# A hybrid DeltaNet / gMLP block on one core: the first MLP product's operands in two fp16 parts in place of two float32r parts

## The chip, the core and the metric

The kernel runs as one launch on one core of one Trainium2 chip. The metric is the device time of that launch in microseconds (us), lower is better. TensorE (PE in the profile) multiplies; VectorE (DVE), ScalarE (ACT) and GpSimd (POOL) do the elementwise work; SyncE (SP) issues every DMA of this kernel, in one queue and in program order.

## What is computed

One block of a diffusion backbone on 128 context rows and 2048 latent rows of width 1024, that is 17 row tiles of 128. Cut to what matters here:

```python
h = rmsnorm(x, norm_mix) * (1 + sc1) + sh1
o = mixer(h, ...)                  # projections, chunked DeltaNet scans (both directions), gMLP, output projection
x = x + ga1 * o
h = rmsnorm(x, norm_ffn) * (1 + sc2) + sh2
x = x + ga2 * (square(relu(h @ w_ff1)) @ w_ff2)     # w_ff1: 1024 x 4096, w_ff2: 4096 x 1024
y = rmsnorm(x, norm_final)
```

All inputs and outputs are float32. The change is in `h @ w_ff1`, the first MLP product.

## The kernel before, in words

Single matmuls do not keep enough bits, so every large product is made of three: each operand is split into a high part and a low part (the rest), and `mm3` (L296, its three matmuls are L301, L302 and L303) adds high x high, high x low and low x high in PSUM. The input projections hold the parts as float16 (`split16`, L202; two parts in one tile), after both operands were scaled by powers of two that the chip works out from bounds of the data (`powers`, L221). The output projection and both MLP products hold them as float32r, unscaled, in two tiles.

The program has five stages that follow one another on TensorE:

1. The input projections with the convolution, block by block (to about 410 us), and the modulation vectors, whose weights pass through the four `raw` buffers of pool `sp` (`NS = 4`).
2. A lead-in to the scan. The last block's decay values `gcol` are transposed (L767), stored to `g_d` (L772), and loaded again as row tiles `gb` (L1082). From these ACT makes the decay matrix E (L1144), POOL and DVE the matrix that is to be inverted, DVE its first transposed factor Y (L1178), and the first product of the inversion on TensorE is L1196, `Y,AH`. Meanwhile TensorE does "fill": the projections of gate, u and v with the rows `hrow` as stationary and the fp16 weights `w` as moving operand. At most `NF = 54` steps of fill stand ahead of the scan.
3. The forward scan over 17 tiles (to about 850 us), with fill between its steps.
4. The backward scan (to about 1190 us), with the output projection as fill, and for rows 9 to 16 the second RMSNorm (`h2_steps`). That makes, for every pair of row tiles, seven combinations of the rows (Strassen's: `put`, L991), splits each in two and stores the parts to `hop_d` (L998).
5. The MLP. The first product runs as 2 x 16 units (`Unit`) of seven combinations each: a unit loads its w_ff1 block, forms the seven combinations of the weights, splits each (`split4`, L1635: ACT cast L1638, DVE subtraction L1632), and multiplies with the loaded `hop` tiles, 12 matmuls of 128x512 a combination. Weights are made `LEAD = 6` combinations ahead. Results leave PSUM by ACT copies (L1707, L1711, L1718, L1735) or DVE additions. The context tile has no pairs; its 64 steps (`context_steps`) run among the units of the second half. Then comes the second product in the same manner.

The order on each engine isn't that of the code. The code gives each step a time (`at`, `spread`, with the scan tile as unit), and the scheduler of the language orders the instructions of each engine by its own estimate. On the chip each engine runs its list in order, so that an instruction that waits holds up all behind it. On SP a load waits there for its buffer too.

Of the kernel before, what the change touches and what calls it, by code (L numbers as in the profile page):

```python
# [62 lines left out]
def hybrid_step(  # L63
# [20 lines left out]
    def f32(ap):  # L84
        return ap.bitcast(F32)
# [20 lines left out]

        return dst[tiles].rearrange("a p d -> p a d")

    hop_d = {(g, o): dp.tile([P, 4, 2, 4, P], F32, name=f"hop_{g}_{o}_d") for g in range(2) for o in range(1, 8)}
# [103 lines left out]
    done = {}  # L213
    phase = {}
    scales = cp.tile([P, 32], F32, name="scales")
    power, under, st3, uses = scales[:, 0:7], scales[:, 7:14], scales[:, 14:20], scales[:, 20:25]
    group = {1: 0, 0: 1, 2: 2, "g": 3, "v": 4, "u": 5, "ab": 6}
    def largest(out, src, axis=mybir.AxisListType.X):
# [26 lines left out]

# [118 lines left out]
    with ExitStack() as ph:  # L364
# [417 lines left out]
        def second_mods():  # L782

            load(out=wsT, in_=w_spatialT)
            V.tensor_copy(wscale[:, 0:4], vec[:, 68:69].to_broadcast([P, 4]))
            mrow = wp.tile([32, P], F32, tag="w", name="mrow4")
            load(out=mrow, in_=mod_d[:, 3 * D : 5 * D].rearrange("c (a b) -> c a b", b=P))
            pc = pt()
            T.transpose(pc[:, 0:32], mrow, ident[:32, :32])
            pc4 = pc[:, 0:32].rearrange("p (c a k) -> p c a k", c=2, a=2)  # L790
            V.tensor_copy(b2, pc4[:, :, 0, :])
            for cd in range(2):
                V.scalar_tensor_tensor(out=a2[:, cd, :], in0=pc4[:, cd, 1, :], scalar=1.0, in1=vec[:, 24:32],
                                       op0=ALU.add, op1=ALU.mult)

        mods = [st for jc in range(4, 10) for st in mod_steps(jc, p1)]
        blk, xs_, cols = prep_block(0)
# [145 lines left out]
    def h2_steps(t, psum, tmp, wide=w512, part=None, half=None, src=None):  # L943
# [1 line left out]

        u = {}
        cd = cond(t)
        wide, part, half = wide, part or wide, half or w512

        def rows():  # L950
            u["x"] = [wide("x"), wide("x")]
# [88 lines left out]
    def hop_tile(dt, n):  # L1040

        side, bufs = ("A", 2) if n else ("B", 5)
        return hops[side].tile([P, 4, 2, 4, P], dt, tag="hop", name="hop", bufs=bufs)

    def hop_next():
        g, o = hop_order.pop(0)
        hop[g, o] = t = hop_tile(F32R, o in ORDER[:2])
        for k in range(0, 4, 2):
            load(out=f32(t)[:, k : k + 2], in_=hop_d[g, o][:, k : k + 2])


    with ExitStack() as ph:
# [355 lines left out]
        def fpart(name):  # L1408
            return fp.tile([P, 512], F32, tag="part", name=name, bufs=5)

        def fhalf(name, dt):
            return sp.tile([P, 512], dt, tag="raw", name=name)


        WO = []
# [215 lines left out]
    def add(out, a, b, op=ALU.add):  # L1631
        V.tensor_tensor(out=out, in0=a, in1=b, op=op)  # L1632

    def split4(src, name="w"):

        h = wp.tile([P, 4, P], F32R, tag="w", name=name + "H")
        lo = wp.tile([P, 4, P], F32R, tag="w", name=name + "L")
        A.copy(h, src)  # L1638
# [11 lines left out]
    class Unit:  # L1650
# [14 lines left out]
        def weights(self, o):  # L1665

            a, w, t = self.raw, self.w, self.t
            if o == 1:
                w[1] = split4(a[0, 0])
            elif o == 5:  # L1670
                t["s"] = as4(w512("s"))
                add(t["s"], a[1, 0], a[1, 1])
                w[5] = split4(t["s"])
            elif o == 6:
                add(t["s"], t["s"], a[0, 0], ALU.subtract)
                w[6] = split4(t["s"])
            elif o == 7:
                d = as4(w512("d"))
                add(d, a[0, 0], a[1, 0], ALU.subtract)
                w[7] = split4(d)  # L1680
            elif o == 3:
                add(t["s"], a[0, 1], t["s"], ALU.subtract)
                w[3] = split4(t["s"])
            elif o == 2:
                w[2] = split4(a[0, 1])
            else:
                w[4] = split4(a[1, 1])

        def product(self, o, onto=None):
            if onto is None:  # L1690
# [11 lines left out]
        def step(self, o):  # L1702
            ps, t = self.ps, self.t
            if o == 1:
                self.product(1)
                t["x"] = w512("x")
                A.copy(t["x"], ps[1])  # L1707
            elif o == 5:
                self.product(5)
                t["p5"] = w512("p5")  # L1710
                A.copy(t["p5"], ps[5])  # L1711
            elif o == 6:
                self.product(6)
                add(t["x"], ps[6], t["x"])
            elif o == 7:
                self.product(7)
                t["z22"] = z = w512("p7")
                A.copy(z, ps[7])  # L1718
                add(z, z, t["x"])
                add(z, z, t["p5"])  # L1720
                rl2(z, z)
                self.out(1, 1, z)
            elif o == 3:
                self.product(3, 5)
                c = w512("c12")
                add(c, ps[5], t["x"])
                rl2(c, c)
                self.out(0, 1, c)
                t["s1"] = w512("s1")
                add(t["s1"], c, t["z22"])  # L1730
                self.keep(s1_d, t["s1"])
            elif o == 2:
                self.product(2, 1)
                c = w512("c11")
                A.activation(c, ps[1], AF.Relu)  # L1735
                A.activation(c, c, AF.Square)
                self.out(0, 0, c)
                s2 = w512("s2")
                add(s2, t["s1"], c, ALU.subtract)
                self.keep(s2_d, s2)  # L1740
            elif o == 4:
                self.product(4, 7)
                c = w512("c21")
                add(c, ps[7], t["x"])
                rl2(c, c)
                self.out(1, 0, c)

    def first_load():
        for i in range(2):
            r = as4(w512("x0"))  # L1750
            load(out=r, in_=h2_d[0][:, i * 4 : i * 4 + 4, :])
            h, lo = split4(r, "x")
            x0.extend((h[:, k, :], lo[:, k, :]) for k in range(4))

    def context_steps(m):
# [5 lines left out]
            u["raw", m] = raw_w(w_ff1[0, k * P : (k + 1) * P, fb * 512 : fb * 512 + 512])  # L1761

        def split():
            u["w", m] = split_w(u.pop(("raw", m)))

        def product():
            if k == 0:
                u["ps"] = bank()
            mm3(u["ps"], [x0[k] + u.pop(("w", m))], first=k == 0, last=k == KT - 1)
            if k == KT - 1:  # L1770
                u["r", fb] = w512("r0")
                A.activation(u["r", fb], u["ps"], AF.Relu)
# [405 lines left out]
```

## Time and profile before

| | us |
|---|---|
| median of 3 runs | 2526.11 (2523.6 to 2528.16) |
| the profiled execution | 2525.39 |
| its span, first to last instruction | 2523.7 |
| TensorE busy | 2482.3 (98%) |
| VectorE busy | 1865.2 (74%) |
| ScalarE busy | 1267.1 (50%) |

The clock granted to TensorE is 0.996 of full speed over the span. Matmuls are pipelined: the duration of one in the profile (some 380 ns for 512 columns) is longer than the distance between the starts of two that follow each other, so a stage's rate is read from the starts in the timeline, and a busy share near 100% can hide short gaps.

### The profile page before, as it was taken

The page shows a single profiled execution, that of the slowest core. Times are in us where ns is not written, and L with a number is a line of the kernel's source. Part 1 is how long each engine was busy: PE and PEld are TensorE (multiplying, and loading weights), DVE is VectorE, ACT ScalarE, POOL GpSimd, SP SyncE. Part 2 cuts the span into 40 slices and gives each one's busy share as a digit, 9 for nine tenths or more (in the row PEclk, how much of TensorE's full clock was granted, in tenths as well). Part 3 has the DMA queues.
Part 4 walks back from the last instruction along what each step waited for, and adds up shares of the span by engine and source line. Part 5 has one row for each costly group of instructions (what it writes and reads, how often), then busy time and mean ns, then how long its engine had stood idle before and what let it go on. Part 6 is the DMA issues. An engine that isn't in the chain of part 4 may idle for free.

```text
span 2523.7 us, 44015 instructions
## 1 busy us (share of the span) xinstructions
PE 2482.3 (98%) x15182; PEld 1917.2 (76%) x15182; DVE 1865.2 (74%) x3877; ACT 1267.1 (50%) x3129; POOL 231.9 (9%) x428
## 2 busy tenths in 40 slices
PE   9999999999999999999999999999999999999998
PEld 4666667666666787788888888888888888888887
DVE  4868886877778889886678878777775557685775
ACT  3756764555556667753455535444343333243442
POOL 3112212211111111110000000000000000000000
PEclk9999999999999999999999999999999999999999
DMA  8766756544444658785977899666589979786773
GB/s 293 231 182 212 226 162 192 178 150 135 129 145 156 217 172 272 260 268 174 313 225 238 249 313 297 188 192 181 145 287 374 324 262 332 243 261 203 225 265 109
DMA packets 479334, 566.61 MB, mean 225 GB/s; under 512 B 37684, under 2 KB 284764, under 8 KB 475526
## 3 DMA queue, kind: packets, MB, share of 16 engines
q1 hardware_dynamic: 479110, 563.80, 68.8%
q8 instruction: 119, 1.95, 0.3%
q14 instruction: 105, 0.86, 0.1%
HBM read 392.90 MB, written 170.76 MB: 223 GB/s over the span
## 4 chain that ended last, share of the span: by engine, by line
PE 84%; DVE 7%; DMA 4%; ACT 2%; issue 1%; SPq 1%; POOL 1%; POOLq 0%; DVEq 0%; ACTq 0%
PE f L301 16%; PE f L303 16%; PE f L302 16%; PE pj L301 6%; PE pj L302 6%; PE pj L303 6%; PE pd L1116 4%; DMA QK<-qk_d 2%; PE pm L301 1%; PE pm L303 1%; PE pm L302 1%; PE pt L671 1%; DMA raw<-in_w_ff_dram 1%; PE pt L630 1%; PE pm L425 1%
## 5 line engine op out<-in xcount | busy, mean ns | idle before, releaser
L301 PE MATMUL f<-hop,zH 128*128 128x512 f32 (+1 forms) x976 | 376.2, 386 | 1.2 <-ACT zH L1638 1.2
L302 PE MATMUL f<-hop,zH 128*128 128x512 f32 (+1 forms) x976 | 376.1, 386 | 0.0
L303 PE MATMUL f<-hop,zL 128*128 128x512 f32 (+1 forms) x976 | 376.1, 386 | 0.0
L301 PE MATMUL f<-hop,wH 128*128 128x512 f32 x896 | 349.7, 391 | 1.6 <-ACT p L1711 1.4
L302 PE MATMUL f<-hop,wH 128*128 128x512 f32 x896 | 348.7, 389 | 0.0
L303 PE MATMUL f<-hop,wL 128*128 128x512 f32 x896 | 347.3, 389 | 0.0
L1638 ACT CAST zH<-zraw 128x512 fp32r<-128x512 f32 x240 | 146.9, 621 | 294.0 <-DMA zraw<-s_d 92.4
L301 PEld LDWEIGHTS f<-hop,zH 128*128 128x128 f32 x976 | 183.3, 188 | 38.6 <-ACT zH L1638 1.6
L303 PEld LDWEIGHTS f<-hop,zL 128*128 128x128 f32 x976 | 183.3, 188 | 37.2 <-DVE zL L1632 0.4
L302 PEld LDWEIGHTS f<-hop,zH 128*128 128x128 f32 x976 | 183.3, 188 | 36.9 <-issue 0.2
L1632 DVE TENSOR_TENSOR zL<-zraw,zH 128x512 fp32r<-128x512 f32 x240 | 162.8, 687 | 65.3 <-ACT zH L1638 53.5
L301 PEld LDWEIGHTS f<-hop,wH 128*128 128x128 f32 x896 | 168.2, 188 | 37.2 <-ACT p L1711 2.3
L303 PEld LDWEIGHTS f<-hop,wL 128*128 128x128 f32 x896 | 168.2, 188 | 35.2
L302 PEld LDWEIGHTS f<-hop,wH 128*128 128x128 f32 x896 | 168.3, 188 | 34.6
L301 PE MATMUL pj<-kH,w 128*128 128x386 f16 (+2 forms) x568 | 180.3, 321 | 6.0 <-ACT w L205 3.3
L302 PE MATMUL pj<-kL,w 128*128 128x386 f16 (+2 forms) x568 | 181.2, 322 | 0.0
L303 PE MATMUL pj<-kH,w 128*128 128x386 f16 (+2 forms) x568 | 180.1, 321 | 0.0
L181 POOL TENSOR_TENSOR r<-rsq,nhalf 128x1 f32<-128x1 f32 (+1 forms) x37 | 25.2, 682 | 1386.4 <-DVE rsq L180 1386.4
L1638 ACT CAST wH<-s 128x512 fp32r<-128x512 f32 x96 | 59.4, 621 | 123.3 <-DVE s L1632 116.8
L617 DVE SCALAR_TENSOR_TENSOR cv<-pj,vec,cv 128x384 f32<-128x384 f32 (+2 forms) x142 | 82.9, 588 | 26.7 <-ACT cv L615 25.5
L301 PE MATMUL pj<-w,hrow 128*128 128x512 f16 x248 | 94.0, 379 | 0.0
L303 PE MATMUL pj<-w,hrow 128*128 128x512 f16 x248 | 94.0, 379 | 0.0
(447 smaller groups left out, 5526.0 us busy)
## 6 DMA issues: line engine op xcount, KB each, us to landing
zraw<-z_d SPq DMA_DIRECT2D x212, 256.0 KB
raw<-in_w_ff_dram SPq DMA_DIRECT2D x192, 256.0 KB
hop<-hop_d SPq DMA_DIRECT2D x28, 1024.0 KB
z_d<-c SPq DMA_DIRECT2D x96, 256.0 KB
zraw<-s_d SPq DMA_DIRECT2D x96, 256.0 KB
raw<-in_w_mod_dram SPq DMA_DIRECT2D x80, 256.0 KB
r<-in_w_ff_dram SPq DMA_DIRECT2D x80, 256.0 KB
s_d<-s SPq DMA_DIRECT2D x64, 256.0 KB
```

The costliest lines, as they stand in the source:

```text
L181: G.tensor_tensor(out=out, in0=t[:np_, :n], in1=nhalf[:np_, :n], op=ALU.pow)
L301: T.matmul(ps, lh, rh, start=first and i == 0, stop=False, skip_group_check=more)
L302: T.matmul(ps, lh, rl, start=False, stop=False, skip_group_check=more)
L303: T.matmul(ps, ll, rh, start=False, stop=last and i == n - 1, skip_group_check=more)
L425: T.matmul(pm[0:2, :], scond[:, k, :], raws[k], start=k == 0, stop=k == KT - 1)
L617: V.scalar_tensor_tensor(out=cv, in0=ps[:, w : w + ncol - 2], scalar=convw[:, w, j : j + 1], in1=cv, op0=ALU.mult, op1=ALU.add)
L630: T.transpose(pq[:, i * P : (i + 1) * P], u["x2"][i], ident)
L671: T.matmul(ps[:, i * P : (i + 1) * P], kTt[:, i * P : (i + 1) * P], rhs[i], start=True, stop=True)
L1116: T.matmul(p[:, h, :], lhs[:, h, :], rhs[:, h, :], start=True, stop=True)
L1632: V.tensor_tensor(out=out, in0=a, in1=b, op=op)
L1638: A.copy(h, src)
```

## The change

Both operands of the first MLP product are split into float16 parts instead of float32r parts, and are scaled for that:

- The rows' scale: `second_mods` takes the largest absolute values of the modulation tables `a2` and `b2`, makes a power of two of them (`four_sum_power`, `powers`: two small matmuls, some column operations on DVE) and multiplies `a2` and `b2` by it.
- The weights' scale: all of w_ff1 is read once more, in 64 loads of 256 KB through the same four `raw` buffers of pool `sp`, and ACT squares each in place with the row sums added up (`square_w1`). `w1_range` then makes the power of two.
- A weight combination is split by an ACT activation with a scale column and a DVE scalar_tensor_tensor (`split16x4`), in place of the ACT cast and the DVE subtraction. Both parts share one tile.
- PSUM is scaled back where it leaves: ACT copies get a scale column, DVE additions become scalar_tensor_tensor (`add_scaled`).
- `put` stores both parts, now 2 bytes an element, with one DMA of 256 KB in place of two of 256 KB. A `hop` tile now holds the parts for both halves of the rows, so that the second half's load no longer waits for a buffer.
- The products' number and shapes stay: 2688 matmuls of 128x512 in the units and 192 in the context steps.

The core of the diff:

```diff
-    hop_d = {(g, o): dp.tile([P, 4, 2, 4, P], F32, ...
+    hop_d = {(g, o): dp.tile([P, 4, 2, 4, P], F16, ...
+    def square_w1(n, raw):
+        A.activation(raw, raw, AF.Square, accum_out=w1_sums[:, n : n + 1])
+
+    def four_sum_power(s, r, top, psum, squared):
+        V.tensor_scalar_mul(top, top, 16.0 if squared else 4.0)
+        powers(s, r, top, 1, psum, squared)
...
+            largest(parts[:, 0:1], a2, mybir.AxisListType.XY)
+            largest(parts[:, 1:2], b2, mybir.AxisListType.XY)
+            V.scalar_tensor_tensor(out=top, in0=parts[:, 0:1], scalar=32.0, in1=parts[:, 1:2], op0=ALU.mult, op1=ALU.add)
+            four_sum_power(h2_power, h2_under, top, pt, False)
+            V.tensor_scalar_mul(a2, a2, h2_power)
+            V.tensor_scalar_mul(b2, b2, h2_power)
...
-            h, lo = half("opH", F32R), half("opL", F32R)
-            A.copy(h, src)
-            V.tensor_tensor(out=lo, in0=src, in1=f32(h), op=ALU.subtract)
-            for i, piece in enumerate((h, lo)):
-                store(out=dst[:, i], in_=f32(piece).rearrange("p (k d) -> p k d", k=4))
+            pair = half("op")
+            A.copy(pair[:, 0, :], src)
+            V.tensor_tensor(out=pair[:, 1, :], in0=src, in1=pair[:, 0, :], op=ALU.subtract)
+            store(out=dst, in_=pair.rearrange("p i (k d) -> p i k d", k=4))
...
+        def w1_load(n):
+            k, fb = divmod(n, 8)
+            w1_raws[n] = raw_w(w_ff1[0, k * P : (k + 1) * P, fb * 512 : fb * 512 + 512], sp, "raw")
...
+        for n in range(64):
+            at(0.5 + n * 0.24, lambda n=n: w1_load(n))
+            at(1.0 + n * 0.24, lambda n=n: square_w1(n, w1_raws.pop(n)))
+        at(16.5, w1_range, "fill")
...
+    def split16x4(src, scale=None):
+
+        t = wp.tile([P, 2, 4, P], F16, tag="w", name="w16")
+        h, lo = t[:, 0], t[:, 1]
+        if scale is None:
+            A.copy(h, src)
+            add(lo, src, h, ALU.subtract)
+        else:
+            A.activation(h, src, AF.Copy, scale=scale)
+            V.scalar_tensor_tensor(out=lo, in0=src, scalar=scale, in1=h, op0=ALU.mult, op1=ALU.subtract)
+        return h, lo
...
+    def add_scaled(out, ps, b):
+        V.scalar_tensor_tensor(out=out, in0=ps, scalar=mlp_under, in1=b, op0=ALU.mult, op1=ALU.add)
...
-                w[1] = split4(a[0, 0])
+                w[1] = split(a[0, 0])
...
-                A.copy(t["x"], ps[1])
+                A.activation(t["x"], ps[1], AF.Copy, scale=mlp_under)
...
-                add(t["x"], ps[6], t["x"])
+                add_scaled(t["x"], ps[6], t["x"])
```

In the code the 64 loads and squares are spread over the forward scan. The scheduler puts them earlier: all 64 stand between the last block of the projections and the first steps of the scan. Three places show it.

On TensorE, in the lead-in, at the transposes of the decay values `gcol` (`hrow` is stationary fill, `w` its moving weights). Before:

```order
L301 LDWEIGHTS hrow
L301 MATMUL pm<-w_2997,hrow 128x512
L767 MATMUL pt<-ident,gcol 128x128
L768 MATMUL pt<-ident,gcol 8x128
L302 LDWEIGHTS hrow
L302 MATMUL pm<-w_2997,hrow 128x512
```

Changed (L313 to L315 are the three matmuls of `mm3`, L779 and L780 the two transposes):

```order
L314 LDWEIGHTS hrow
L314 MATMUL pj<-w_3244,hrow 128x512
L779 MATMUL pt<-ident,gcol 128x128
L780 MATMUL pt<-ident,gcol 8x128
L315 LDWEIGHTS hrow
L315 MATMUL pj<-w_3244,hrow 128x512
```

111 fill matmuls stand before the first scan product `Y,AH` in both. Before, 25 of them stand ahead of `gcol` and 86 behind it; now 92 stand ahead and 19 behind.

On SP, from the store of the decay values to the loads of `gb`. Before:

```order
L772 DMA g_d<-scr 128x128
L773 DMA g_d<-scr 8x128
L1369 DMA gate_d<-th 128x512
L635 DMA vt_d<-tk 128x2x128 x3
L1082 DMA gb<-g_d 128x512 x2
```

Changed (L187 are the new loads of w_ff1):

```order
L187 DMA raw<-in_w_ff_dram 128x512 x3
L784 DMA g_d<-scr 128x128
L785 DMA g_d<-scr 8x128
L373 DMA hrow<-h_d 128x768 x2
L647 DMA vt_d<-tk 128x2x128
L1391 DMA gate_d<-th 128x512
L647 DMA vt_d<-tk 128x2x128
L373 DMA hrow<-h_d 128x768 x2
L647 DMA vt_d<-tk 128x2x128
L373 DMA hrow<-h_d 128x768 x5
L1104 DMA gb<-g_d 128x512 x2
```

Nine loads of `hrow` now stand between the store and the loads that read it back, and 40 of the 64 new loads stand ahead of the store.

On ACT, from the first steps of the scan's first two tiles (L1144/L1166 make E, L1170/L1192 cast AH, L1212/L1234 and L1213/L1235 take Y and X out of PSUM). Before:

```order
L1170 CAST AH<-KK 128x512
L1344 ACTIVATE gw<-pm,scales 128x512
L1347 ACTIVATE gw<-gw,scales 128x512
L1344 ACTIVATE gw<-pj,scales 128x512
L1212 CAST Y<-pd 128x16x16
L1213 CAST X<-pd 128x16x16
```

Changed (L247 are the new squares):

```order
L1192 CAST AH<-KK 128x512
L247 ACTIVATE raw,w_sums<-raw 128x512 x3
L1366 ACTIVATE gw<-pm,scales 128x512
L247 ACTIVATE raw,w_sums<-raw 128x512 x4
L1369 ACTIVATE gw<-gw,scales 128x512
L247 ACTIVATE raw,w_sums<-raw 128x512 x3
L1366 ACTIVATE gw<-pj,scales 128x512
L247 ACTIVATE raw,w_sums<-raw 128x512
L1234 CAST Y<-pd 128x16x16
L1235 CAST X<-pd 128x16x16
```

Eleven squares now stand between this cast of AH and the next Y. In all, 40 squares stand ahead of the first E of the scan and 24 behind it.

More of the change, by code (lines that the diff above doesn't have):

```diff
@@ L107, in by_tiles @@
         return dst[tiles].rearrange("a p d -> p a d")
-    hop_d = {(g, o): dp.tile([P, 4, 2, 4, P], F32, name=f"hop_{g}_{o}_d") for g in range(2) for o in range(1, 8)}
+    hop_d = {(g, o): dp.tile([P, 4, 2, 4, P], F16, name=f"hop_{g}_{o}_d") for g in range(2) for o in range(1, 8)}
     z_d = [dp.tile([4 if a else 1, P, 2, NK, P], F32, name=f"z{a}_d") for a in range(5)]
@@ L215, in hybrid_step @@
     scales = cp.tile([P, 32], F32, name="scales")
+    w1_sums = cp.tile([P, 64], F32, name="w1_sums")
+    h2_power, h2_under, w1_power, w1_under, mlp_under = (scales[:, i : i + 1] for i in range(25, 30))
     power, under, st3, uses = scales[:, 0:7], scales[:, 7:14], scales[:, 14:20], scales[:, 20:25]
@@ L289, in w512, with pair16 @@
         return wp.tile([P, 512], dt, tag="w", name=name)
+    def pair16(name):
+        return wp.tile([P, 2, 512], F16, tag="w", name=name)
     def wrow(row):
@@ L794, in second_mods @@
                                        op0=ALU.add, op1=ALU.mult)
+            top8 = smp.tile([P, 8], F32, tag="topc", name="toph", bufs=1)
+            top, parts = top8[:, 0:1], top8[:, 3:5]
+            largest(parts[:, 0:1], a2, mybir.AxisListType.XY)
[4 more added lines that the diff above has]
+            V.tensor_scalar_mul(b2, b2, h2_power)
         mods = [st for jc in range(4, 10) for st in mod_steps(jc, p1)]
@@ L947, in h2_steps @@
         cd = cond(t)
-        wide, part, half = wide, part or wide, half or w512
+        wide, part, half = wide, part or wide, half or pair16
         def rows():
@@ L1042, in hop_tile @@
         side, bufs = ("A", 2) if n else ("B", 5)
-        return hops[side].tile([P, 4, 2, 4, P], dt, tag="hop", name="hop", bufs=bufs)
+        shape = [P, 2, 4, 2, 4, P] if dt == F16 else [P, 4, 2, 4, P]
+        return hops[side].tile(shape, dt, tag="hop", name="hop", bufs=bufs)
     def hop_next():
         g, o = hop_order.pop(0)
-        hop[g, o] = t = hop_tile(F32R, o in ORDER[:2])
+        if g == 0:
+            both = hop_tile(F16, o in ORDER[:2])
+            hop[0, o], hop[1, o] = both[:, 0], both[:, 1]
         for k in range(0, 4, 2):
-            load(out=f32(t)[:, k : k + 2], in_=hop_d[g, o][:, k : k + 2])
+            load(out=hop[g, o][:, k : k + 2], in_=hop_d[g, o][:, k : k + 2])
     with ExitStack() as ph:
@@ L1409, in fpart, with fhalf, w1_range @@
             return fp.tile([P, 512], F32, tag="part", name=name, bufs=5)
-        def fhalf(name, dt):
-            return sp.tile([P, 512], dt, tag="raw", name=name)
+        def fhalf(name):
+            return sp.tile([P, 2, 512], F16, tag="raw", name=name)
+        w1_raws = {}
+        def w1_load(n):
+            k, fb = divmod(n, 8)
+            w1_raws[n] = raw_w(w_ff1[0, k * P : (k + 1) * P, fb * 512 : fb * 512 + 512], sp, "raw")
+        def w1_range():
+            top = smp.tile([P, 8], F32, tag="topc", name="topw", bufs=1)[:, 0:1]
+            row = sp.tile([P, 512], F32, tag="raw", name="row1")
+            V.memset(row[0:8, 0:P], 1.0)
+            phase["ones"] = row[:, 0:P]
+            V.tensor_reduce(out=top, in_=w1_sums, axis=mybir.AxisListType.X, op=ALU.max)
+            four_sum_power(w1_power, w1_under, top, pj, True)
+            V.tensor_tensor(out=mlp_under, in0=w1_under, in1=h2_under, op=ALU.mult)
         WO = []
@@ L1679, in weights @@
                 add(d, a[0, 0], a[1, 0], ALU.subtract)
-                w[7] = split4(d)
+                w[7] = split(d)
             elif o == 3:
                 add(t["s"], a[0, 1], t["s"], ALU.subtract)
-                w[3] = split4(t["s"])
+                w[3] = split(t["s"])
             elif o == 2:
-                w[2] = split4(a[0, 1])
+                w[2] = split(a[0, 1])
             else:
-                w[4] = split4(a[1, 1])
+                w[4] = split(a[1, 1])
         def product(self, o, onto=None):
@@ L1710, in step @@
                 t["p5"] = w512("p5")
-                A.copy(t["p5"], ps[5])
+                A.activation(t["p5"], ps[5], AF.Copy, scale=mlp_under)
             elif o == 6:
                 self.product(6)
-                add(t["x"], ps[6], t["x"])
+                add_scaled(t["x"], ps[6], t["x"])
             elif o == 7:
@@ L1717, in step @@
                 t["z22"] = z = w512("p7")
-                A.copy(z, ps[7])
+                A.activation(z, ps[7], AF.Copy, scale=mlp_under)
                 add(z, z, t["x"])
@@ L1725, in step @@
                 c = w512("c12")
-                add(c, ps[5], t["x"])
+                add_scaled(c, ps[5], t["x"])
                 rl2(c, c)
@@ L1734, in step @@
                 c = w512("c11")
-                A.activation(c, ps[1], AF.Relu)
+                A.activation(c, ps[1], AF.Relu, scale=mlp_under)
                 A.activation(c, c, AF.Square)
@@ L1763, in split @@
         def split():
-            u["w", m] = split_w(u.pop(("raw", m)))
+            u["w", m] = split16(u.pop(("raw", m)), w1_power)
         def product():
@@ L1771, in product @@
                 u["r", fb] = w512("r0")
-                A.activation(u["r", fb], u["ps"], AF.Relu)
+                A.activation(u["r", fb], u["ps"], AF.Relu, scale=mlp_under)
         def turn():
```

9 lines of the change are left out of this document (5 added, 4 removed).

## The prediction

> **What bounds the kernel now.** I read the page's busy times first, then the table of stages, the groups of matmuls in the first MLP product, and the timeline of TensorE's starts. The page:
>
> ```profile
> span 2523.7 us, 44015 instructions
> PE 2482.3 (98%) x15182; PEld 1917.2 (76%) x15182; DVE 1865.2 (74%) x3877; ACT 1267.1 (50%) x3129; POOL 231.9 (9%) x428
> ```
>
> The table by stage (lead-in, both scans, first MLP product, second; columns: length, then busy us and instructions of each engine, granted clock, DMA share, GB/s):
>
> ```profile
> 391.00:468.00 77.00, 76.72 (x581) 49.60 (x580) 52.32 (x163) 37.72 (x115) 22.45 (x16) 1.00 0.67 210
> 410.00:850.00 440.00, 429.89 (x3845) 287.47 (x3844) 336.61 (x956) 249.41 (x672) 74.45 (x84) 1.00 0.51 159
> 850.00:1180.00 330.00, 320.23 (x2749) 267.21 (x2750) 269.96 (x672) 209.73 (x664) 51.37 (x62) 1.00 0.71 235
> 1192.00:1860.00 668.00, 666.35 (x2987) 550.91 (x2986) 505.85 (x826) 316.81 (x617) 5.72 (x9) 1.00 0.74 232
> ```
>
> From 1192 to 1860 us TensorE is busy 666 of 668 us, at clock 1.00. The groups there say with what, and that almost nothing makes it wait (after the last bar: its idle time):
>
> ```profile
> L301 PE MATMUL f<-hop,wH 128*128 128x512 f32 x896 | 349.7, 391 | 1.6 <-ACT p L1711 1.4 <-DMA hop<-hop_d 0.2
> L301 PE MATMUL f<-wH,xH 128*128 128x512 f32 x64 | 25.5, 399 | 0.0
> ```
>
> With L302 and L303 that is 3 x 896 + 3 x 64 = 2880 matmuls of 128x512 in float32r. A duration of 391 ns isn't their rate; the starts are. Two rows of the timeline, 149 matmuls apart, and below them two of the fp16 fill in the lead-in, 63 apart, same shape, both at clock 1.00:
>
> ```profile
> 1466.10 0.39 PE L302 MATMUL f<-hop,wH 128*128 128x512 f32 x1
> ...
> 1499.92 0.39 PE L301 MATMUL f<-hop,wH 128*128 128x512 f32 x1
> ```
>
> ```profile
> 429.83 0.38 PE L303 MATMUL pm<-w,hrow 128*128 128x512 f16 x1
> ...
> 443.43 0.38 PE L303 MATMUL pm<-w,hrow 128*128 128x512 f16 x1
> ```
>
> 33.82 / 149 = 227.0 ns for float32r, 13.60 / 63 = 215.9 ns for float16. So this stage is paced by the matmul stream itself: 2880 x 0.227 = 654 of its 668 us.
>
> **The change, part by part.**
>
> *The products in fp16.* Their number stays, each start comes 227.0 - 215.9 = 11.1 ns sooner: 2880 x 11.1 ns = 32.0 us gained, if nothing else becomes the limit.
>
> *Splits and evictions in that stage* get a scale column. The rows to compare (cast and scaled activation; DVE subtraction and scalar_tensor_tensor; a PSUM copy and a PSUM activation with scale column):
>
> ```profile
> L1638 ACT CAST wH<-raw 128x512 fp32r<-128x512 f32 x95 | 57.7, 619 | 0.3 <-PE f L303 0.3
> L205 ACT ACTIVATE w<-raw,scales 128x512 f16<-128x512 f32 x48 | 31.8, 718 | 0.7 <-DVE w L206 0.5
> L1632 DVE TENSOR_TENSOR wL<-raw,wH 128x512 fp32r<-128x512 f32 x95 | 64.6, 684 | 11.6 <-ACT wH L1638 11.6
> L206 DVE SCALAR_TENSOR_TENSOR w<-raw,scales,w 128x512 f16<-128x512 f32 x48 | 34.0, 741 | 1.5 <-ACT w L205 1.5
> L1711 ACT COPY p<-f 128x512 f32<-128x512 f32 x32 | 18.8, 586 | 32.4 <-PE f L303 28.4 <-DVE wL L1632 4.0
> L1344 ACT ACTIVATE gw<-pm,scales 128x512 f32<-128x512 f32 x17 | 11.7, 690 | 7.7 <-PE pm L303 7.4 <-DVE bst L1375 0.2
> 1325.00:1350.00 25.00, 25.00 (x116) 20.69 (x115) 22.34 (x40) 13.35 (x30) 0.55 (x1) 1.00 0.71 226
> ```
>
> ACT: 288 splits x 99 ns = 28.5 us, 136 evictions x 104 ns = 14 us. DVE: 288 x 57 ns = 16.4 us, and 96 additions out of PSUM, for which I take the same 57 ns, 5.5 us. In a stage of 668 - 32 = 636 us ACT goes from 317 to 359 us (56%), DVE from 506 to 528 us (83%). Both stay under TensorE, and weights are made six combinations (16 us) ahead: I take 0. If that cover is gone, it is in places like the last row above, where DVE is busy 22.3 of 25 us; 22.3 x 1.04 in 25 x 0.952 us is 97%. Bound: +5.
>
> *64 loads and 64 squares in the lead-in.* Nothing like it stands there now. The prices: an accumulating square of 128x512 (two starts in a row), a 256 KB load in quiet and in dense traffic (the chain of waits, from issue to landing), and the traffic of 385 to 470 us, in 40 slices:
>
> ```profile
> 40.16 0.63 ACT L252 ACTIVATE junk<-raw 128x512 bf16<-128x512 f32 x1
> ...
> 40.91 0.63 ACT L252 ACTIVATE junk<-raw 128x512 bf16<-128x512 f32 x1
> ```
>
> ```profile
> 592.63 2.93 DMA QK<-qk_d
> ...
> 960.96 6.21 DMA QK<-qk_d
> ```
>
> ```profile
> GB/s 10 123 121 63 183 65 151 108 242 122 103 211 235 251 282 264 289 354 250 182 102 97 194 305 384 295 318 404 400 400 368 326 265 2 0 0 0 112 248 18
> ```
>
> ACT: 64 x 0.755 = 48 us on top of 37.7 in 77 us. DMA: 210 GB/s x 77 us = 16.2 MB, plus 64 x 0.262 = 16.8 MB, 33.0 MB; at the best slice, 404 GB/s, that needs 82 us. Each alone asks for 5 to 9 us more than there is. The Trainium skill's page "DMA: Bandwidth & Descriptors" (Specifications) gives about 358 GB/s as the limit of HBM for a core; by it 33.0 MB would need 92 us, 15 more than there is. The slices at 400 and 404 speak against it, and the sum goes by them.
>
> What decides is the order of the instructions. The transposes of `gcol` start a chain (store, load of `gb`, E, the matrix, Y) that the first scan product waits for:
>
> ```profile
> 424.21 0.27 PE L767 MATMUL pt<-ident,gcol 128*128 128x128 f32 x1
> ...
> 443.65 0.28 PE L1196 MATMUL pd<-Y,AH 128*128 128x64 f16 x4
> ```
>
> ```profile
> 441.35 0.70 DVE L1178 STREAM_TRANSPOSE Y<-X 128x512 f16<-128x512 f16 x1
> ```
>
> ```profile
> 425.46 0.22 PE pt L630 x2
> ```
>
> Y is there at 442.05, 17.8 us after `gcol`. Now 86 fill matmuls (18.6 us) stand between, and TensorE comes 1.6 us after Y: the chain is hidden. In the changed order only 19 stand between (4.1 us) and three pairs of transposes (0.7 us), because the other 67 went ahead of `gcol`. TensorE then stands for 17.8 - 4.8 = 13.0 us. The fill is limited and its order fixed, so nothing gives this back later.
>
> On SP, nine loads of `hrow` now stand between the store and the load of `gb`:
>
> ```profile
> 415.76 2.81 SPq L361 DMA_DIRECT2D hrow<-h_d x6
> 426.19 3.78 SPq L635 DMA_DIRECT2D vt_d<-tk x3
> ```
>
> 9 x 0.47 = 4.2 us, in part while SP would stand at the `vt_d` stores anyway (3.78 now): +2, between -3.8 (that stand is over by then) and +4.2. The 24 squares behind the first E (18 us of ACT, eleven in a row ahead of one Y) and the loads ahead of `hrow` block in order: +3, between 0 and the 12 us that ACT and DMA lack at worst. Lead-in in all: 13 + 2 + 3 = +18, between 9 and 29.
>
> *The two powers of two.* Each is two small matmuls with DVE work between them; the order puts 18 or more fill matmuls between the two: 0, at most 1 each.
>
> *Half the bytes to `hop_d`* in the backward scan, 28 stores of 256 KB in place of these 56:
>
> ```profile
> hop_d<-opH SPq DMA_DIRECT2D x28, 256.0 KB
> hop_d<-opL SPq DMA_DIRECT2D x28, 256.0 KB
> DVE QK L1216 <- DMA QK<-qk_d: 20.8, 11, 2.9
> ```
>
> That is 7.3 MB of the stage's 235 GB/s x 330 us = 77.6 MB, and DVE waits there 20.8 us for QK loads. 9.5% of that is 2 us: -2, between 0 and -8, since the QK load queues mostly behind other loads.
>
> *Sum:* -32 + 18 - 2 + 0 = -16, from the profiled execution's 2525.4 (span 2523.7 and 1.7 around it) to 2509.4. The median of the runs lies 0.7 above it: 2510. Bounds: -32 - 8 + 9 = -31, and -32 + 29 + 5 + 2 = +4: 2495 to 2530.
>
> **The rivals.**
>
> *The staging buffers pace the lead-in (slower).* A new load waits for the square four loads earlier, and SP with it. A round of four takes the landing time, an issue (0.3) and a square (0.755). At 2.93 us that is 16 x 4.0 = 64 us, which fits in 77; at 6.21 us it is 16 x 7.3 = 117 us, 40 more than there is, and all loads of the scan stand behind it: -32 - 2 + 40 = +6, 2532. It decides against the change from a round of (77 + 32) / 16 = 6.8 us on. For it: bytes in the lead-in double, and with 0.67 it is busy already. Against: TensorE's stand of 13 us is time for it. Chance 0.18.
>
> *The lead-in costs nothing:* the chain after `gcol` is short enough on the chip, or TensorE reaches `gcol` earlier than the order suggests. -34 + 1, 2492. Against it stand the 19 matmuls of cover. 0.12.
>
> *The change doesn't do what it says:* the fp16 rate of the fill doesn't hold for `hop`, whose 512 columns are four pieces, while the fill's lie in one. Then +16, 2541. Against it:
>
> ```profile
> 1182.73 0.39 PE L301 MATMUL pj<-wH,oH 128*128 128x512 f32 x1
> ...
> 1191.80 0.39 PE L302 MATMUL pj<-wL,oH 128*128 128x512 f32 x1
> ```
>
> In float32r the output projection, with columns in one piece, starts 40 matmuls in 9.07 us, 226.8 ns each, like the units. 0.04.
>
> *An fp16 stream far faster than the fill's.* It would have to be paced by something that the fill doesn't show; no row does. The Trainium skill's page "TensorE: Matmul & The Clock Gate" (Back-to-back issue gap) gives 216 ns at 512 columns for one matmul after another, which the trace agrees with (215.9), and about 131 ns for a sustained stream of weight loads and matmuls, which it does not. By the second the gain would be 2880 x 96 ns = 276 us, 2249. 0.01.
>
> **How the numbers follow.** The forecast has 0.65, the rivals the rest. 0.2% of this kernel is 5 us, about what a measurement can tell from no change. Faster by more: 0.58 of the forecast's 0.65, 0.05 of the first rival, the second and the fourth whole, 0.76. Within: 0.05 and 0.04, 0.09. Slower: 0.02, 0.09 and the third's 0.04, 0.15. The range leaves out the third and fourth rival, the upper half of the first and the forecast's and the second's edges, together under 0.2: 2493 to 2531.
>
> **What would show it right or wrong.** In the changed profile: 216 ns between starts of the units' matmuls, and a first MLP product of about 636 us; some 13 us or more in which TensorE waits ahead of the first `Y,AH`, with the later stages' lengths nearly kept; all squares done early in the scan. The sum is wrong if the lead-in's stand is under 9 or over 29 us, if the units' starts stay at 227 ns, or if DVE holds TensorE up in the units.

## The result, and the profile after

| | before | after |
|---|---|---|
| median of 4 runs, us | 2527.14 (2523.6 to 2532.5) | 2553.43 (2552.52 to 2554.16) |
| span of the profiled execution | 2523.7 | 2551.3 |
| granted TensorE clock | 0.996 | 0.988 |

The ratio is 1.0102, 95% interval 1.0083 to 1.0121: the change makes the kernel 26 us slower, where 16 us faster was forecast. One execution of those below, of e12_rows_power_fixed, ran at a granted clock of 0.849 and took 2787.75 us; it is left out of the medians. The page of after, its first two lines of busy time:

```profile
span 2551.3 us, 44102 instructions
PE 2468.6 (97%) x15188; PEld 1664.4 (65%) x15188; DVE 1888.3 (74%) x3898; ACT 1342.8 (53%) x3257; POOL 235.7 (9%) x429
```

TensorE is busy 13.7 us less than before and yet the span is 27.6 us longer. The table by stage says where (lead-in, both scans, first MLP product; columns as in the prediction's table, windows moved to where the stages now lie):

```profile
391.00:513.00 122.00, 87.51 (x593) 52.89 (x592) 54.97 (x176) 77.06 (x245) 22.46 (x15) 0.87 0.84 266
455.00:895.00 440.00, 402.05 (x3635) 269.07 (x3634) 327.09 (x932) 257.25 (x700) 63.38 (x82) 0.97 0.53 166
895.00:1225.00 330.00, 324.31 (x2778) 269.82 (x2776) 273.90 (x680) 213.42 (x670) 52.19 (x63) 1.00 0.64 207
1236.00:1884.00 648.00, 637.16 (x2985) 294.93 (x2984) 522.20 (x822) 352.38 (x616) 8.19 (x9) 0.99 0.68 207
```

What took 77 us takes 122, and TensorE is busy in 87.5 of them. The starts of the Y factor, one for each scan tile, give the same without windows: the first stands 35.1 us later than before (476.4 for 441.4), the fourth 45.2 later, and then the distance stays, 45.4 at the last tile of the forward scan. So 45 us go into the lead-in and the first three tiles, and nothing more into the forward scan. By stages, from one first instruction to the next:

| | before | after | forecast | found |
|---|---|---|---|---|
| Y of the fourth tile starts | 487.5 | 532.7 | +18 | +45.2 |
| from there to the first unit | 704.7 | 703.9 | -2 | -0.8 |
| first MLP product | 667.7 | 647.2 | -32 | -20.5 |
| second product, to the end | 663.7 | 667.5 | 0 | +3.8 |

In the lead-in, the timeline of the chain that the prediction priced at 17.8 us, across the engines:

```profile
449.75 0.33 PE L779 MATMUL pt<-ident,gcol 128*128 128x128 f32 x1 [0.54 <-ACT tk L646]
456.74 0.38 SPq L784 DMA_DIRECT2D g_d<-scr  x1
464.29 0.91 SPq L1104 DMA_DIRECT2D gb<-g_d  x2
469.38 1.28 ACT L1166 ACTIVATE E<-gb,gcol 128x128 f32<-128x128 f32 x4 [8.79 <-DMA gb<-g_d]
476.41 0.70 DVE L1200 STREAM_TRANSPOSE Y<-X 128x512 f16<-128x512 f16 x1
477.16 0.37 PE L1218 MATMUL pd<-Y,AH 128*128 128x64 f16 x4 [21.57 <-DVE Y L1200]
```

`gcol` itself comes at 449.75 in place of 424.21, 25.5 us later. From there to the start of Y it was 17.1 us and is 26.7: the store to `g_d` stands 7.0 us behind the transposes (0.7 before), since loads of w_ff1 are ahead of it on SP, and the load of `gb` another 7.5 (5.1 before). TensorE has used up its fill by then and stands 21.57 us.

In the first MLP product the waits on TensorE are these:

```profile
PE f L313 <- ACT p L1768: 7.8, 1, 7.8
PE f L1000 <- DVE x L993: 2.4, 1, 2.4
PE f L313 <- DVE tmp L1524: 0.8, 1, 0.8
```

The rate is what was forecast. Two starts of units, 95 matmuls apart:

```profile
1300.55 0.38 PE L313 MATMUL f<-hop,w 128*128 128x512 f16 x1
...
1321.05 0.38 PE L315 MATMUL f<-hop,w 128*128 128x512 f16 x1
```

20.50 / 95 = 215.8 ns (215.9 forecast). What is missing of the 32 us is one stand. The timeline around it, SP, ACT and TensorE in order of time:

```profile
1488.79 0.66 ACT L1015 CAST op<-y 128x512 f16<-128x512 f32 x1
1494.85 0.77 SPq L1006 DMA_DIRECT2D h_d<-ev  x1
1499.28 0.32 SPq L1808 DMA_DIRECT2D x<-h_d  x1
1499.69 0.38 SPq L1006 DMA_DIRECT2D h_d<-ev  x1
1502.53 0.62 ACT L1680 CAST w<-x 128x512 f16<-128x512 f32 x1 [13.08 <-DMA x<-h_d]
1503.41 0.32 SPq L1808 DMA_DIRECT2D x<-h_d  x1
1506.74 0.62 ACT L1680 CAST w<-x 128x512 f16<-128x512 f32 x1 [3.59 <-DMA x<-h_d]
1507.26 0.68 ACT L1768 ACTIVATE p<-f,scales 128x512 f32<-128x512 f32 x1
1507.99 0.59 PE L313 MATMUL f<-hop,w 128*128 128x512 f16 x1 [7.82 <-ACT p L1768]
1508.37 0.63 PE L314 MATMUL f<-hop,w 128*128 128x512 f16 x1
...
1512.21 0.46 PE L314 MATMUL f<-hop,w 128*128 128x512 f16 x1
1512.51 0.38 PE L315 MATMUL f<-hop,w 128*128 128x512 f16 x1
```

These are the context tile's rows, `x0`. They are stored to DRAM in two halves (L1006) and loaded again (L1808); each load is issued only 4.4 and 3.7 us after the store that it reads. Their splits stand on ACT's in-order list with the loads not yet there, and behind them stands the eviction `p` that TensorE needs. The same stand was there before, at 0.5 us: ACT waited 7.1 and 1.7 us for these two loads, TensorE 0.49 us for the `p` behind them. (The other 0.9 of the 1.4 us at `p` lie 70 us later.) After the stand of 7.8 us the matmuls start 9 x 0.427 us apart (1508.37 to 1512.21) and only then 0.22 apart, 2 us more. The Trainium skill's page "TensorE: Matmul & The Clock Gate" (What's actually happening; Wait — 56ns, not 53.3ns?) says that the array runs at half its clock after an idle window of some 3.4 us, with 426.7 ns between starts at 512 columns, and 215.7 when warm: the trace agrees with both figures.

### The profile page after: what moved, and what is told of

Read it like the earlier page. It is cut to its first block, busy times and chain, and to the rows that moved or that the text cites. A ratio compares the mean times of both kernels' runs of the same rounds, so it can differ in the third digit from the quotient of the medians.

```text
span 2551.3 us, 44102 instructions
## 1 busy us (share of the span) xinstructions
PE 2468.6 (97%) x15188; PEld 1664.4 (65%) x15188; DVE 1888.3 (74%) x3898; ACT 1342.8 (53%) x3257; POOL 235.7 (9%) x429
## 4 chain that ended last, share of the span: by engine, by line
PE 79%; DMA 8%; DVE 6%; ACT 4%; issue 1%; SPq 1%; POOL 1%; POOLq 0%; DVEq 0%; ACTq 0%
PE f L313 16%; PE f L314 16%; PE f L315 16%; PE pj L313 5%; PE pj L315 5%; PE pj L314 5%; PE pd L1138 5%; DMA raw<-in_w_ff_dram 2%; PE pm L313 2%; PE pm L314 2%; PE pm L315 2%; DMA QK<-qk_d 1%; PE pt L683 1%; DMA raw<-in_w_mod_dram 1%; DMA t_d<-r 1%
## 5 line engine op out<-in xcount | busy, mean ns | idle before, releaser
L313 PE MATMUL f<-hop,zH 128*128 128x512 f32 (+1 forms) x976 | 376.8, 386 | 2.1 <-ACT zH L1691 2.1
L315 PE MATMUL f<-hop,zL 128*128 128x512 f32 (+1 forms) x976 | 376.7, 386 | 0.4 <-DVE zL L1673 0.4
L313 PE MATMUL f<-hop,w 128*128 128x512 f16 x896 | 340.3, 381 | 8.6 <-ACT p L1768 7.8
L314 PE MATMUL f<-hop,w 128*128 128x512 f16 x896 | 341.2, 381 | 0.0
L315 PE MATMUL f<-hop,w 128*128 128x512 f16 x896 | 339.8, 381 | 0.0
L314 PEld LDWEIGHTS <-w 128*128 128x128 f16 x1536 | 151.3, 99 | 154.3 <-issue 16.1
L313 PEld LDWEIGHTS <-w 128*128 128x128 f16 x1536 | 151.1, 98 | 147.7 <-issue 3.8
L315 PEld LDWEIGHTS <-w 128*128 128x128 f16 x1536 | 151.2, 98 | 145.0 <-issue 3.5
L313 PEld LDWEIGHTS f<-hop,zH 128*128 128x128 f32 x976 | 183.4, 188 | 40.8 <-ACT zH L1691 3.8
L315 PEld LDWEIGHTS f<-hop,zL 128*128 128x128 f32 x976 | 183.4, 188 | 39.6 <-DVE zL L1673 2.9
L313 PE MATMUL pj<-kH,w 128*128 128x386 f16 (+2 forms) x568 | 181.1, 323 | 6.3 <-ACT w L205 3.3
L315 PE MATMUL pj<-kH,w 128*128 128x386 f16 (+2 forms) x568 | 180.1, 321 | 0.0
L181 POOL TENSOR_TENSOR r<-rsq,nhalf 128x1 f32<-128x1 f32 (+1 forms) x37 | 26.7, 720 | 1372.2 <-DVE rsq L180 1372.2
L1683 ACT ACTIVATE w<-s,scales 128x512 f16<-128x512 f32 x96 | 68.5, 717 | 94.5 <-DVE s L1673 94.2
L206 DVE SCALAR_TENSOR_TENSOR w<-raw,scales,w 128x512 f16<-128x512 f32 x112 | 81.9, 745 | 20.3 <-ACT w L205 20.3
L313 PE MATMUL pj<-w,hrow 128*128 128x512 f16 x248 | 94.5, 381 | 0.0
```

The costliest lines, as they stand in the source:

```text
L181: G.tensor_tensor(out=out, in0=t[:np_, :n], in1=nhalf[:np_, :n], op=ALU.pow)
L206: V.scalar_tensor_tensor(out=t[:, 1, :], in0=raw, scalar=scale, in1=t[:, 0, :], op0=ALU.mult, op1=ALU.subtract)
L313: T.matmul(ps, lh, rh, start=first and i == 0, stop=False, skip_group_check=more)
L314: T.matmul(ps, lh, rl, start=False, stop=False, skip_group_check=more)
L315: T.matmul(ps, ll, rh, start=False, stop=last and i == n - 1, skip_group_check=more)
L1683: A.activation(h, src, AF.Copy, scale=scale)
```

## The experiments

Theory at the start: the 64 loads and squares, in the in-order lists of SP and ACT ahead of the first scan chain, are the whole lead-in loss (A). Rivals: `gcol`'s place behind the fill costs its 13 us by itself, as the prediction had it, and the pass the rest (B); the bytes cost their time wherever they stand (C). "Pass" means the 64 loads and 64 squares. Each run's ratio is to runs of the kernel before on the same chip.

| run | median us | ratio, 95% interval |
|---|---|---|
| e1_no_pass | 2519.27 | 0.9972, 0.9961 to 0.9982 |
| e2_pass_in_before | 2556.90 | 1.0115, 1.0100 to 1.0130 |
| e3_pass_spread | 2521.49 | 0.9977, 0.9966 to 0.9988 |
| e4_gcol_early | 2538.52 | 1.0044, 1.0027 to 1.0060 |
| e5_squares_only | 2528.68 | 1.0000, 0.9990 to 1.0011 |
| e6_loads_only | 2543.86 | 1.0064, 1.0046 to 1.0083 |
| e7_spread_and_mended | 2502.39 | 0.9901, 0.9872 to 0.9931 |
| e8_other_pool | 2556.76 | 1.0117, 1.0094 to 1.0140 |
| e9_no_pass_mended | 2500.17 | 0.9889, 0.9872 to 0.9905 |
| e10_small_loads | 2528.57 | 1.0001, 0.9991 to 1.0011 |
| e11_x0_alone | 2542.33 | 1.0059, 1.0044 to 1.0074 |
| e12_rows_power_fixed | 2506.15 | 0.9919, 0.9899 to 0.9939 |

**e1_no_pass.**

```diff
-        for n in range(64):
-            at(0.5 + n * 0.24, lambda n=n: w1_load(n))
-            at(1.0 + n * 0.24, lambda n=n: square_w1(n, w1_raws.pop(n)))
+        at(0.5, lambda: V.memset(w1_sums, 0.64))
```

> The changed kernel without the 64 loads and 64 squares; the table of row sums is filled with a fixed 0.64 instead (that part of the computation is left out). The order on TensorE stays as in the changed kernel, gcol behind the fill. Theory A (the loads and squares, standing in the in-order lists of SP and ACT ahead of the first scan chain, are the whole +45 us of the lead-in): Y of the first scan tile starts at about 441 us as before the change, total 2553 - 45 = 2508. Theory B (the place of gcol behind the fill costs 13 us by itself, as the prediction had it, the pass the rest): Y at about 454, total 2521. Theory C (the traffic of the pass): as A here, 2508.

2519.27, theory B. The timeline:

```profile
433.72 0.27 PE L779 MATMUL pt<-ident,gcol 128*128 128x128 f32 x1
451.79 0.70 DVE L1200 STREAM_TRANSPOSE Y<-X 128x512 f16<-128x512 f16 x1
452.55 0.37 PE L1218 MATMUL pd<-Y,AH 128*128 128x64 f16 x4 [7.86 <-DVE Y L1200]
```

Without the pass the chain is back at 18.1 us (17.1 before), but `gcol` is still 9.5 us late and every Y of the forward scan 10.2 to 10.5. So the pass costs 2553.4 - 2519.3 = 34 us, and something else in the change 10 to 13. The expectation was wrong in one point: the order on TensorE does not stay. Of the 111 fill matmuls, 65 stand ahead of `gcol` here and 46 behind it, against 92 and 19 in the changed kernel. So the pass itself moves `gcol` too. The 40 matmuls more than before take 40 x 0.216 = 8.6 of the 9.5 us.

**e2_pass_in_before.** The kernel before with the same three lines of loads and squares added.

> The kernel before, float32r products and all, plus the 64 loads and 64 squares at the same given times (their sums are used by nothing). Theory A and theory C: the lead-in's +45 us come by themselves, 2527 + 45 = 2572. Theory B: here gcol stands between its two places (39 groups of fill ahead of it, 48 in the changed kernel, 25 before), so that a part of the 13 us is missing: about 2563. If the loss needs the fp16 part: 2527.

2556.90: +30.4 with float32r products. The pass costs its time without any fp16 in the kernel. Theory A's 45 is out; B had forecast 2563. (In the trace 39 fill matmuls stand ahead of `gcol`, as expected, but in the changed kernel it is 92, not 48.)

**e3_pass_spread.**

```diff
-            at(1.0 + n * 0.24, lambda n=n: square_w1(n, w1_raws.pop(n)))
+            at(1.0 + n * 0.24, lambda n=n: calm(lambda: square_w1(n, w1_raws.pop(n))))
```

> The changed kernel with each square ordered on ACT behind the scan step that its time stands for, so that loads and squares are spread over the forward scan, about four for each scan tile; all bytes and all squares stay. Theory A: the 45 us go and little comes back in the scan (ACT has 25 idle us in 100 there): 2508 to 2513. Theory B: 13 us stay at the first Y,AH: 2521. Theory C (16.8 MB cost their time wherever they stand): the lead-in is short but the scan grows by 30 to 45 us: 2540 to 2553.

2521.49. The same bytes and squares, at other places, cost 2 us in place of 34: theory C falls. In the traced execution Y starts with e1's at the first tile and falls 4.7 us behind over the forward scan (tile 16 at 767.4 for 762.7). SP stands long in it:

```profile
SPq L187 <- ACT raw L247: 68.9, 39, 4.0
```

That costs at most the 2 to 5 us above. That what stands behind these loads on SP is wanted later still is the likely reason; it wasn't tried.

**e4_gcol_early.** The last three of the four gate tiles of fill are ordered on TensorE behind the two transposes of `gcol`.

```diff
...
+            st = st if g == 0 else lambda st=st: after_gcol(st)
...
```

> The changed kernel with the transposes of gcol ahead of the last three of the four gate tiles of fill, about where they stand in the kernel before; the 64 loads and squares stay where they are. Theory A: SP and ACT still hold the chain up and gcol's place gives at most its few us: 2545 to 2553. Theory B: 13 us come back and the stand ahead of the first Y,AH falls from 21.6 to about 9 us: 2540. A third case: gcol's place is most of the 45 us: 2515.

2538.52, 15 us less, theory B again; 24 fill matmuls stand ahead of `gcol` here. The stand ahead of the first `Y,AH` falls to 6.4 us:

```profile
PE pd L1220 <- DVE Y L1202: 6.4, 1, 6.4
```

**e12_rows_power_fixed** asks why `gcol` is late without the pass. To e1 it adds:

```diff
-            largest(parts[:, 0:1], a2, mybir.AxisListType.XY)
-            largest(parts[:, 1:2], b2, mybir.AxisListType.XY)
...
-            four_sum_power(h2_power, h2_under, top, pt, False)
+            V.memset(h2_power, 64.0)
+            V.memset(h2_under, 1.0 / 64.0)
```

> As e1_no_pass (no loads, no squares), and the rows' power of two is a fixed 64 in place of the one worked out from a2 and b2, so that its two small matmuls and the work of VectorE between them are left out too. In the written order the transposes of gcol then stand again after about as much fill as in the kernel before. If the 10 us that gcol's place costs come from this small chain in the list of TensorE (priced at 0 to 1 us in the prediction): gcol at about 425 us, Y at 442, total 2519 - 10 = 2509. If gcol's place on the chip is set by something else: 2519.

2506.15:

```profile
422.20 0.27 PE L779 MATMUL pt<-ident,gcol 128*128 128x128 f32 x1
440.02 0.70 DVE L1196 STREAM_TRANSPOSE Y<-X 128x512 f16<-128x512 f16 x1
```

`gcol` and Y are back where they were: Y is 11.8 us earlier than in e1, the median 13 us lower. 23 fill matmuls stand ahead of `gcol` here, 65 in e1. The rows' power of two, two small matmuls (0.27 and 0.38 us in e1) with a little work of DVE between them, costs some 12 us by moving `gcol` behind the fill. It takes one of three PSUM buffers (`pt`) that the transposes of `gcol` take too; that this is why they moved is argued and wasn't tried apart.

**e5_squares_only and e6_loads_only** part the 34 us of the pass. e5:

```diff
-            at(0.5 + n * 0.24, lambda n=n: w1_load(n))
-            at(1.0 + n * 0.24, lambda n=n: square_w1(n, w1_raws.pop(n)))
+            at(1.0 + n * 0.24, lambda n=n: square_w1(n, w1_raws[0], w1_raws[1]))
```

> The changed kernel with the 64 squares at the same given times, but all of one buffer that holds a fixed 0.0354 and with no load (the bound is then a fixed number). It parts the 35 us that the pass costs on top of gcol's place. Theory A1 (ACT's 48 us in its in-order list are it): 2519 + 35 = 2554, less what ACT no longer waits for loads, 2540 to 2554. Theory A2 (the loads are it: SP standing for a buffer, and traffic ahead of the scan's own loads): 2519 to 2524. The rival of the prediction, a round of four buffers, needs both and gives 2519 to 2524 here too.

e6 keeps the line with `w1_load` and leaves out the one with `square_w1`.

> The changed kernel with the 64 loads through the four buffers, but no square reads them (the table is filled with a fixed 0.64). A load waits then only for the load four earlier to land. Theory A1: 2519 to 2524. Theory A2 with traffic as the cause: 2540 to 2554. The rival of the prediction (a load waits for the square four earlier): loads go at the landing time alone, so 2519 to 2530.

2528.68 and 2543.86: the squares alone cost 9.4 us over e1, the loads alone 24.6, together 34.0, and both as one 34.2. Neither A1 nor A2 holds alone. That the sum comes out so exactly is in part luck. By the ratios of the table, each to the kernel before on its own chip, the three are 7, 23 and 33 us. And the time is not lost at the same places (us later than in e1):

| | `gcol` | Y of the first tile | Y of the fourth tile |
|---|---|---|---|
| e5, squares alone | 4.7 | 9.3 | 9.0 |
| e6, loads alone | 12.8 | 22.9 | 26.3 |
| after, both | 16.0 | 24.6 | 34.7 |

At the first Y the two overlap by 8 us. The changed kernel loses 10 more behind it: 27.7 us pass there between the second and the third Y, 16.1 in e1, and from 489.7 to 501.2 us of it ACT has the eleven squares that stand ahead of one Y. In e5 no square stands there: all 64 are done by 456.5 us, before the scan's first AH. So e5 does not show what the squares cost at the places where the changed kernel has them. It also has 82 fill matmuls ahead of `gcol`, e1 65; these 17 are 3.7 of its 4.7 us at `gcol`.

The table by stage, 420 to 450 us of e5 and 450 to 480 us of e6:

```profile
420.00:450.00 30.00, 25.58 (x139) 14.48 (x137) 8.13 (x27) 29.46 (x93) 11.24 (x1) 1.00 0.55 177
```

```profile
450.00:480.00 30.00, 10.95 (x53) 5.01 (x52) 4.97 (x10) 5.13 (x14) 2.31 (x3) 0.68 1.01 345
```

In e5 ACT is busy 29.5 of 30 us; in e6 ACT is free, and the DMA engines are at 1.01 of their time with 345 GB/s. In e6 no load waits for a square, and 25 of 34 us stay; the prediction's first rival, read as its expectation has it, would give 2530 at most. The loads on SP, in after and in e6 (durations in ns, smallest, median and largest, then the first and the last start):

```profile
L187 SPq DMA_DIRECT2D raw<-in_w_ff_dram x64: 327/330/1922, 390.3 to 508.3; - x64
```

```profile
L187 SPq DMA_DIRECT2D raw<-in_w_ff_dram x64: 327/346/1162, 389.9 to 497.1; - x64
```

That is 118.0 us in after, 7.4 for a round of four, and 107.2 in e6, 6.7 a round. So the rounds stay long without the squares: from 388 to 515 us SP stands 27.7 us for squares in after, and 30.0 us for loads to land in e6. The four buffers can pace the loads either way, and e6 takes only the square out of the round. More buffers at these places weren't tried, so that this rival isn't excluded.

**e10_small_loads** asks whether the loads cost by their number on SP or by their bytes. To e6:

```diff
-            w1_raws[n] = raw_w(w_ff1[0, k * P : (k + 1) * P, fb * 512 : fb * 512 + 512], sp, "raw")
+            w1_raws[n] = sp.tile([P, 512], F32, tag="raw", name="raw")
+            load(out=w1_raws[n][:, 0:64], in_=w_ff1[0, k * P : (k + 1) * P, fb * 512 : fb * 512 + 64])
```

> As e6_loads_only, with 64 loads, but each of 64 columns in place of 512, so 32 KB and not 256 KB (the pass is left out all the same). SP has as many instructions to issue, the bytes fall to an eighth. If the 25 us of the loads are SP's list (64 issues and the stand for a buffer ahead of the stores and loads of the scan's chain): 2535 to 2544. If they are the bytes, 16.8 MB where the transfers already stand at 0.6 to 0.9: 2519 to 2524.

The loads on SP:

```profile
L1441 SPq DMA_DIRECT2D raw<-in_w_ff_dram x64: 327/418/1434, 391.5 to 476.5; - x64
```

2528.57, between the two: with an eighth of the bytes 9.3 of the 24.6 us stay, 15.3 go. The order of the loads on SP changes a little with their size, and 59 fill matmuls stand ahead of `gcol` for 70 in e6, so these two are rough. With the bytes the rounds of four buffers shorten too: the 64 loads are out in 85.0 us. The waits on TensorE in the lead-in, e6 and e10:

```profile
PE pd L1218 <- DVE Y L1200: 19.0, 1, 19.0
PE pt L801 <- DMA mrow<-mod_d: 8.9, 1, 8.9
```

```profile
PE pd L1218 <- DVE Y L1200: 12.7, 1, 12.7
PE pt L801 <- DMA mrow<-mod_d: 2.3, 1, 2.3
```

The first place where the bytes show is not the scan's chain: a transpose of `mrow`, ahead of `gcol` on TensorE, waits 8.9 us for its load. In after it doesn't wait; there TensorE stands 5.5 us in seven other places up to `gcol`.

**e11_x0_alone.** In the changed kernel, `x0`'s splits ten steps after the loads:

```diff
...
         if p == half - 20:
             first_load()
+        if p == half - 10:
+            first_split()
...
```

> The changed kernel, nothing left out, with one edit: the splits of the context rows' x0 parts ten steps after their loads. If the stand of 7.8 us and the slower clock behind it are a cost of their own: 2553 - 9 to 10 = 2544, and a first MLP product of 638 us in place of 647. If the stand only moves to the next thing that waits: 2550 to 2553.

2542.33, 11 us less, and the first product takes 636.5 us, the 636 of the prediction:

```profile
1237.00:1874.00 637.00, 633.01 (x2982) 293.64 (x2982) 521.58 (x821) 352.46 (x616) 8.18 (x9) 1.00 0.69 210
```

ACT 352 and DVE 522 us, 359 and 528 forecast: the one wait of TensorE for a scaled split or eviction there is 0.7 us.

**e7_spread_and_mended** is the changed kernel with the edits of e3, e4 and e11 together, and nothing left out.

> The changed kernel, nothing left out, with three changes of order: squares spread over the scan as in e3_pass_spread, gcol ahead of three of the four gate tiles as in e4_gcol_early, and the splits of the context rows' x0 parts, on which ACT stood 16.7 us and TensorE 7.8 us in the first MLP product, asked for ten steps later than their loads. By the parts: 2521 - 10 (gcol) - 9 (the wait of 6.9 and some 2 at a lower clock after it) = 2502. If gcol's and the pass's costs aren't additive: 2508 to 2515. If another wait takes the place of the x0 one: 2511.

2502.39: 0.9901 of the kernel before (0.9872 to 0.9931), faster than both, and the 2502 that was expected. The three edits measured singly in the changed kernel come to more, though: 32 (e3), 15 (e4) and 11 (e11) are 58 us, which would give 2495. So the terms overlap by some 7 us: e3 alone already takes the fill ahead of `gcol` from 92 to 59, a part of what e4 does.

**e8_other_pool** spreads in another way: buffers from the weights' pool, no order forced on the squares, the other two edits as in e7.

```diff
-            w1_raws[n] = raw_w(w_ff1[0, k * P : (k + 1) * P, fb * 512 : fb * 512 + 512], sp, "raw")
+            w1_raws[n] = raw_w(w_ff1[0, k * P : (k + 1) * P, fb * 512 : fb * 512 + 512])
```

> As e7_spread_and_mended, but the spreading is done in another way: the loads take their buffers from the large pool of the weights (tag w) in place of the four staging buffers, which ties each load to the buffers that the fill's steps give back; no order is forced on the squares. If the 5 to 10 us that e3_pass_spread loses in the scan come from SP standing for the four buffers (68.9 us of it there): 2495. If they come from the squares on ACT: 2502, as e7_spread_and_mended.

2556.76, a miss by 55 to 62 us. The loads are spread too, over the first thirteen tiles; but ACT's waits from 443 to 740 us are

```profile
ACT raw L247 <- DMA raw<-in_w_ff_dram: 83.8, 47, 4.6
```

where in e7 there is no such wait in that time. In e7 a square stands on ACT long after its load was issued, and SP waits (67.6 us); here it stands where the load hasn't landed, and ACT waits, with the evictions of the inversion behind it: TensorE's wait for the eviction Y grows from 1.4 us in e7 to 22.2 us in that time. Against before, Y is 1.5 us later at the first tile, 53.4 at the tenth and 61.7 at the thirteenth. SP stands here too, 84.2 us for squares. So SP's wait alone cost little in e7, and with ACT's wait beside it 54 us more; that it is ACT's that costs is read from the evictions and wasn't tried apart.

**e9_no_pass_mended** is e7 without the pass.

> As e7_spread_and_mended without the pass: no loads and no squares, the table of row sums filled with a fixed 0.64 (that part is left out). It is what the fp16 products bring when nothing is paid for the weights' bound. If the terms add: 2502 less the 8 us that the spread pass costs in the scan, 2494. If the pass in e7 costs nothing: 2502.

2500.17, 0.9889 (0.9872 to 0.9905): with e7 at 0.9901 the spread pass costs 2 us, not told apart from nothing, and not the 8 expected.

## Why the prediction was wrong, point by point

- **Products in fp16, -32: right.** 215.8 ns a start, and e11 shows a first product of 636.5 us, 31.2 less.
- **Splits and evictions with a scale column, 0: right** for these engines. But the stage was priced by what ACT and DVE do, and a stand that was in the trace of before, 0.5 us at the eviction `p` behind the loads of `x0`, was passed over. It grew to 7.8 us, and 2 us more at the doubled spacing of 427 ns; e11 gives 11 us for it, beyond the bound of +5. Why the loads of `x0` come later against ACT's list than before wasn't tried.
- **The step that failed: the loads and squares in the lead-in, +2 on SP and +3 for "block in order".** They cost 34, beyond the bounds of 4.2 and 12. The prediction had seen 33.0 MB where 82 us are needed at the best rate, and ACT 9 us over; it let both fit into the 13 us in which TensorE would stand anyway. But the stand is at the end of the chain `gcol`, store, `gb`, E, Y, and the loads and squares are ahead of it, within it and behind it. Against e1 they bring `gcol` 16.0 us later, make the chain from there to Y 8.6 us longer (26.7 for 18.1), and cost 10.1 more up to the fourth Y. Apart, the squares cost 9.4 us and the loads 24.6, of which 15 go with the bytes; how the 34 divide at the places where the changed kernel has both stays open.
- **`gcol` behind the fill, 13 us: right in size (12 in e12, 15 in e4), wrong in most of its cause. The two powers of two, 0, at most 1 each: wrong.** They were priced by their own duration, and `gcol`'s place was put down to the loads and squares. In the traces 88 fill matmuls stand behind `gcol` with neither (e12), 46 with the rows' power (e1) and 19 with both; the pass without the power takes 86 to 72 (e2). So the rows' power does the larger part and the pass the rest. The size came out in part by luck. In e1 the cover after `gcol` is larger than counted, so that TensorE stands 7.9 us, not 13. But the stand costs more than its length, which the prediction left out: the granted clock is 0.57 in the 5 us behind it, and what lies between the first two `Y,AH` steps takes 5.0 us in place of 2.9.
- **Half the bytes to `hop_d`, -2:** not told from nothing: the backward scan's Y takes 341.8 us from first to last before, 338.6 after, 341.6 in e12.
- **The first rival, +40 in the lead-in, 2532:** near in size (the pass 34, the lead-in 45), and its mark was passed (a round of 7.4 us, 6.8 to decide). The wait for a square is at most a part: without it 25 of the 34 us stay (e6), but with rounds of 6.7 us. Whether the four buffers pace the lead-in stays open. They can't be all of it, as squares with no load cost 9.4 us (e5).
- **The second product, 0:** +3.8 in after and +2.8 to +5.5 in every kernel with fp16 products, +0.5 in e2. It opens with the DMA engines at 1.02 of their time before and 1.04 after, and TensorE's stands in it grow from 1.2 to 2.5 us. Whether it is less time to load ahead wasn't tried; it stays open.

The sum with the measured terms: -31 (products) + 11 (`x0`) + 12 (rows' power) + 34 (pass) - 1 (scans) + 4 (second product) = +29, measured +26 by the medians and +27.6 in the profiled executions.

## What to carry to other kernels

A time that code gives to side work is a wish: work whose buffers are free goes where the engine looked idle to the scheduler. So tie it to a step of the stage that has the room, on the engine where its wait would hurt, so that the wait falls on the queue whose next work is wanted later; here that was worth 32 us with the same bytes. Price a small step by what it is put ahead of, not by its own length, and side work in front of a serial chain by what it adds to each engine's list in that chain. Here the sum of the parts, 34 us, was much nearer than the 5 that were left after one part had been hidden behind another.

## What was not expected of the hardware

- A stand of 7.8 us on TensorE costs 2 us more: 427 ns between starts for the next 4 us, 215.8 after. The stand of 7.9 us in e1 costs 2.1 us more in the same way.
- A load that reads what a store has just written to DRAM was issued 4.4 and 3.7 us after that store in this trace.
- 64 loads of only 32 KB in the lead-in cost 9 us (e10): each occupies SP 0.33 us at least, 0.42 in the median, some 27 us in all. What their 2.1 MB and the wait for a buffer add wasn't parted from that.
